# A macaron decoder trunk on one core: the opening taken by token tiles, and the final norm's reciprocal root taken by ScalarE

## The chip, the core and the metric

The kernel runs on 1 core of one Trainium2 chip. The metric is the device time of one execution in microseconds (us), the median over runs; lower is better. Engines are named as the profile names them: PE (TensorE matmul), PEld (its weight loads), DVE (VectorE), ACT (ScalarE), POOL (GpSimd), SP (SyncE, which issues most DMAs; SPq is its queue).

## What is computed

Two layers of a decoder trunk on x of 512 tokens by 1024 features, all float32, then a last RMSNorm:

```python
def rms_norm(x, g):
    y = x * lax.rsqrt(jnp.mean(x * x, axis=-1, keepdims=True) + 1e-6)
    return y * g
def swiglu(x, w_in, w_out):          # w_in 1024 x 5632, w_out 2816 x 1024
    g, u = jnp.split(x @ w_in, 2, axis=-1)
    return (jax.nn.silu(g) * u) @ w_out
h = x
for i in range(2):
    h = h + 0.5 * swiglu(rms_norm(h, ffn1_norm[i]), ffn1_w_in[i], ffn1_w_out[i])
    hn = rms_norm(h, mix_norm[i])
    h = h + (recurrent_mixer(hn, ...) if i == 0 else spatial_gating_mixer(hn, ...))
    h = h + 0.5 * swiglu(rms_norm(h, ffn2_norm[i]), ffn2_w_in[i], ffn2_w_out[i])
return rms_norm(h, final_norm)
```

## The kernel before, in words

**Products.** Every large product is a Strassen-like scheme of seven block products (P1, P2, P5, P6, P3, P7, Q4; `seven`), and every block product is made of three fp32r matmuls per tile (128 x 128 by 128 x 512): both operands are split into a high part `hi` and a rest `lo`, and hi*hi, lo*hi and hi*lo are summed in PSUM. The high part of a weight tile (`whi`) is an ACT copy, its rest (`wlo`) a DVE subtraction (`Sub.split`, recorded at L96 and L87). The left operand is x, transposed on PE by matmuls with the identity into PSUM (tiles `e`, L267), then multiplied with the norm's gain while it is read out of PSUM: `hi` by ACT, `lo` by DVE (L93). x's tokens are the left blocks A11, A12, A22, A21: token tiles 0 and 1 or 2 and 3, first or second 512 features. A block has two groups (`first.g[0]`, `first.g[1]`) of two feature tiles (index q) each.

**Order of the work.** The schedule is manual: each engine executes its instructions in the order in which the program writes them. The list `subs` holds one entry for each weight tile of 128 x 1024 with its matmuls; the loop at the end goes through them, splits up to three entries ahead, and runs hooks tied to an entry's number and phase ("pre" and "mid" ahead of its matmuls, "rest" next to them, "end" behind them). Weights come through 8 buffers (`raw`); SP issues their loads in list order.

**The opening** (from L1411). SP issues one load of x's A11 (tiles 0 and 1 together, 512 KB), then the first weight tile as two halves of 256 KB (`raws[0].halves`), the second weight tile, A12, and more weights. PE runs warm-up matmuls on zeros (L1444), turns the gain, runs three more warm-ups, transposes A11 into two PSUM tiles of one bank each, one per group (`turn(0, "A11")`, `turn(1, "A11")`: group 0's tile holds token tiles 0 and 1 of its two feature tiles), and runs one more warm-up. Then come group 0's first feature tile (`part(0, "A11", 0, True)`: high part and rest both by DVE), the first half of the first weight tile, group 0's second feature tile, the second half of the weight; after six matmuls of P1 `other_block` gives group 1's parts and the second weight tile. P1's matmuls are at L369, those of P2 at L381 to L383, those of the FFN's narrow pair (which comes behind P2, subs[4] to subs[11]) at L828. After P1's second half the block's plain values are needed again: at subs[2] "pre" `value(0, "A11", True)` and `value(1, "A11", True)` take A11 out of PSUM by DVE (four instructions of 128 x 256), and at "rest" ACT takes A12 (four of 128 x 256). Both are `a` in the profile.

**The end.** `FinalNorm` squares the finished pieces of x on ACT, takes the root of the mean with AF.Sqrt (`root`; tile `fs`), and `newton` on DVE takes the reciprocal (L944) and refines it in one Newton step; then x is scaled and stored. Ten entries before the end a one-element Sqrt makes ACT load its table.

The inner order of the first product reads:

```python
[(q, i, m, s) for q, i in qs for m in range(3) for s in range(2)] if ci == 0
    else [(q, i, m, s) for m in range(3) for q, i in qs for s in range(2)]
...
if n == (4 if ci else 6):
    opening[ci]()
```

(s is the token tile, q the feature tile, m = 1 takes x's rest, m = 2 the weight's rest.)

Of the kernel before, what the change touches and what calls it, by code (L numbers as in the profile page):

```python
# [52 lines left out]
def trunk(ctx: ExitStack, tc: tile.TileContext, a: dict, out: bass.AP):  # L53
# [57 lines left out]
    class Raw:  # L111


        halves = False

# [17 lines left out]
        def fetch(self):  # L133
            for q in ((slice(0, 1), slice(1, 2)) if self.halves else (slice(0, self.shape[1]),)):
                nc.sync.dma_start(out=self.v[:, q, :], in_=self.src[:, q, :])

        def add(self, src):
# [200 lines left out]
    def seven(block, cuts, left, w, posts, order=None, own=False, apart=False, joined=None, opening=None):  # L338
# [12 lines left out]
        def mm_of(prod, ci):  # L351
# [3 lines left out]
            def mm(sub):  # L355
# [6 lines left out]
                if opening and prod == "P1":  # L362
                    qs = list(enumerate(pairs))
                    for n, (q, i, m, s) in enumerate([(q, i, m, s) for q, i in qs for m in range(3) for s in range(2)]
                                                     if ci == 0 else
                                                     [(q, i, m, s) for m in range(3) for q, i in qs for s in range(2)]):
                        if n == (4 if ci else 6):
                            opening[ci]()
                        nc.tensor.matmul(bk[name, s], left(prod, i, s)[m == 1], (sub.lo if m == 2 else sub.hi)[:, q, :],  # L369
                                         start=(i, m) == (0, 0), stop=(i, m) == (cuts[-1][-1], 2))  # L370
                    for s in range(2 * ci):
                        posts[prod](s, bk[name, s])
                    return
# [524 lines left out]
    class FinalNorm:  # L898
# [32 lines left out]
        def root(self, t, n):  # L931

            g, i = t // 2, t % 2
            if g not in self.s:
                self.s[g] = self.new("fs", 2)
            act(self.s[g][:, i : i + 1], self.q[g, n][:, i : i + 1], AF.Sqrt, bias=self.m[g][:, i : i + 1])

        def newton(self, g, n, i):
# [4 lines left out]
            tt(v, q, m, ALU.add)  # L943
            nc.vector.reciprocal(out=r, in_=r)  # L944
            if w == 1:
# [460 lines left out]

    hook(len(subs) - 10, "rest", lambda: act(tiny(1), vcol(0), AF.Sqrt))

# [7 lines left out]

    def load_x(t0, c0, w=512):
        src = a["x"][0][t0 * P : (t0 + 2) * P, c0 : c0 + w]
        nc.sync.dma_start(out=X[:, t0 : t0 + 2, c0 : c0 + w], in_=src.rearrange("(t p) c -> p t c", p=P))

# [7 lines left out]

    raws[0].halves = True
    load_x(0, 0)  # L1430
    load_more(2)
# [41 lines left out]

    def part(i, name, q, vector=False):

        g, c, gain = first.g[i], slice(q * H, (q + 1) * H), first.src(i, name)[1][q]
        if name not in g.hl:
            g.hl[name] = slot(F32R, "hi"), slot(F32R, "lo")
        hi, lo = (t[:, c] for t in g.hl[name])
        src = opening[i, name][:, c]  # L1480
        if vector:
            ts(hi, src, gain, None, ALU.mult)
        else:
            act(hi, src, AF.Copy, scale=gain)
        stt(lo, src, gain, f32(hi), ALU.mult, ALU.subtract)

    def value(i, name, vector=False):

        g, ps, gains = first.g[i], opening.pop((i, name)), first.src(i, name)[1]
        if name == "A21" or not vector:  # L1490
            g.take(name, ps, gains)
            return
# [12 lines left out]
    def other_block():  # L1505
        parts(1, "A11")
        subs[1].split()

    warm_up(3, 512)
    turn(0, "A11")  # L1510
    turn(1, "A11")
    warm_up(1, 512)
    part(0, "A11", 0, True)
    subs[0].split(lambda: part(0, "A11", 1))
    for n, phase, fn in ((3, "rest", vec_rest),
                         (2, "pre", lambda: (value(0, "A11", True), value(1, "A11", True))),
                         (2, "rest", lambda: (value(0, "A12"), value(1, "A12"))),
# [63 lines left out]
```

## Time and profile before

| | |
|---|---|
| median of 3 runs | 1608.38 us (1608.36 to 1608.82) |
| the profiled execution's own time | 1609.21 us |
| span inside it | 1606.4 us |
| busy share of the span | PE 99%, PEld 83%, DVE 85%, ACT 65%, POOL 14% |
| mean granted TensorE clock | 0.999 |
| ACT table loads | 23 |

The span runs from the first to the last recorded instruction of the profiled execution; 2.8 us of its own time lie around it. Its own time is 0.83 us over the median. A line of the timeline reads: start in us, duration in us, engine, source line, operation, output<-inputs, shape, and the number of equal instructions merged into the line; in brackets how long the engine had been idle before it and whose result ended that. A merged line lasts from the first start to the last end.

### The profile page before, as it was taken

The numbers are of one execution on the slowest core, as the hardware profiler recorded it, in microseconds if no ns is written. First come the engines' busy times: TensorE is split into PE (matmuls) and PEld (weight loads), VectorE is DVE, ScalarE is ACT, GpSimd is POOL, SyncE is SP. The second block draws the span as 40 slices with busy tenths as digits, with TensorE's granted clock in tenths as the row PEclk, the third lists the DMA queues.
The fourth block names the chain that finished last, engine by engine and source line by source line (L and its number), as shares of the span: only waits on it lengthen the run. The fifth ranks groups of instructions, "written<-read, shape, count | busy, mean of one in ns | idle before, by whom it ended". The sixth has DMA issues, their size and how long they took to land.

```text
span 1606.4 us, 20839 instructions
## 1 busy us (share of the span) xinstructions
PE 1598.0 (99%) x7451; PEld 1331.0 (83%) x7451; DVE 1368.8 (85%) x1837; ACT 1036.6 (65%) x1504; POOL 222.3 (14%) x201
## 2 busy tenths in 40 slices
PE   9999999999999999999999999999999999999998
PEld 7888888898888888888888888888888888888886
DVE  6998888888998788878987988878978988879778
ACT  7656556658777556656776565566886766565566
POOL 2111111100011111111101111111211011111110
PEclk9999999999999999999999999999999999999999
DMA  9877876944383886876837768768877657686693
GB/s 289 184 165 166 214 182 153 221 125 112 87 216 83 187 215 156 208 164 161 206 98 182 171 161 214 183 148 213 224 191 193 157 126 189 171 208 160 166 209 97
DMA packets 164263, 279.29 MB, mean 174 GB/s; under 512 B 11472, under 2 KB 37184, under 8 KB 164160
## 3 DMA queue, kind: packets, MB, share of 16 engines
q1 hardware_dynamic: 114656, 184.84, 36.8%
q0 software_dynamic: 47712, 91.30, 34.2%
q10 hardware_dynamic: 1792, 1.84, 0.4%
q8 instruction: 58, 0.95, 0.2%
q14 instruction: 45, 0.37, 0.1%
HBM read 275.84 MB, written 2.10 MB: 173 GB/s over the span
## 4 chain that ended last, share of the span: by engine, by line
PE 98%; DVE 1%; DMA 0%; ACT 0%; issue 0%; SPq 0%; DVEq 0%
PE A L382 14%; PE A L383 14%; PE A L381 14%; PE C L382 8%; PE C L381 8%; PE C L383 8%; PE p L828 5%; PE B L382 4%; PE B L383 4%; PE B L381 4%; PE e L267 4%; PE r L225 2%; PE r L227 2%; PE r L226 2%; PE Q L383 1%; PE Q L382 1%
## 5 line engine op out<-in xcount | busy, mean ns | idle before, releaser
L87 DVE TENSOR_TENSOR wlo<-raw,whi 128x1024 fp32r<-128x1024 f32 (+1 forms) x537 | 640.2, 1194 | 181.9 <-ACT whi L96 176.9
L96 ACT ACTIVATE whi<-raw 128x1024 fp32r<-128x1024 f32 (+1 forms) x537 | 554.9, 1034 | 368.9 <-PE A L382 118.1
L381 PE MATMUL A<-whi,hi 128*128 128x512 f32 x1016 | 399.8, 394 | 0.0
L383 PE MATMUL A<-wlo,hi 128*128 128x512 f32 x1016 | 396.4, 390 | 0.0
L382 PE MATMUL A<-whi,lo 128*128 128x512 f32 x1016 | 396.2, 390 | 0.0
L383 PEld LDWEIGHTS A<-wlo,hi 128*128 128x128 f32 x1016 | 190.8, 188 | 40.0 <-DVE wlo L87 0.4
L382 PEld LDWEIGHTS A<-whi,lo 128*128 128x128 f32 x1016 | 191.0, 188 | 38.4 <-DVE lo L87 0.3
L381 PEld LDWEIGHTS A<-whi,hi 128*128 128x128 f32 x1016 | 191.0, 188 | 38.1
L381 PE MATMUL C<-whi,hi 128*128 128x512 f32 x560 | 218.6, 390 | 0.0
L382 PE MATMUL C<-whi,lo 128*128 128x512 f32 x560 | 218.3, 390 | 0.0
L383 PE MATMUL C<-wlo,hi 128*128 128x512 f32 x560 | 218.2, 390 | 0.0
L138 POOL DMA_DIRECT2D raw<-in_ffn_w_in_dram x82 | 99.1, 1216 | 733.2 <-DVE raw L87 374.3
L138 POOL DMA_DIRECT2D raw<-in_ffn_w_out_dram x72 | 83.4, 1202 | 367.6 <-DVE wlo L87 171.8
L87 DVE TENSOR_TENSOR raw<-raw,raw 128x1024 f32<-128x1024 f32 x108 | 129.9, 1202 | 0.5
L87 DVE TENSOR_TENSOR lo<-a,hi 128x512 fp32r<-128x512 f32 (+1 forms) x188 | 123.4, 663 | 2.2 <-ACT hi L96 2.1
L96 ACT ACTIVATE hi<-a 128x512 fp32r<-128x512 f32 (+1 forms) x188 | 112.0, 601 | 19.6 <-DVE a L87 16.7
L382 PEld LDWEIGHTS C<-whi,lo 128*128 128x128 f32 x560 | 105.2, 188 | 22.3 <-DVE lo L87 0.7
L381 PEld LDWEIGHTS C<-whi,hi 128*128 128x128 f32 x560 | 105.2, 188 | 21.7
L383 PEld LDWEIGHTS C<-wlo,hi 128*128 128x128 f32 x560 | 105.2, 188 | 21.7
L96 ACT ACTIVATE c<-A 128x512 f32<-128x512 f32 x132 | 77.7, 597 | 70.3 <-PE A L383 70.3
L381 PE MATMUL B<-whi,hi 128*128 128x512 f32 x280 | 109.4, 391 | 0.0
L383 PE MATMUL B<-wlo,hi 128*128 128x512 f32 x280 | 109.1, 390 | 0.0
(168 smaller groups left out, 2092.5 us busy)
## 6 DMA issues: line engine op xcount, KB each, us to landing
raw<-in_ffn_w_in_dram SPq DMA_DIRECT2D x161, 512.0 KB, 4.5
raw<-in_ffn_w_out_dram SPq DMA_DIRECT2D x100, 512.0 KB, 5.7
raw<-in_ffn_w_in_dram POOLq DMA_DIRECT2D x82, 512.0 KB, 7.5
raw<-in_ffn_w_out_dram POOLq DMA_DIRECT2D x60, 512.0 KB, 7.8
raw<-in_sg_w_in_dram SPq DMA_DIRECT2D x20, 512.0 KB, 6.7
raw<-in_ffn_w_in_dram SPq DMA_DIRECT2D x34, 256.0 KB, 4.9
raw<-in_rec_w_in_dram SPq DMA_DIRECT2D x16, 512.0 KB, 3.9
raw<-in_sg_w_in_dram POOLq DMA_DIRECT2D x12, 512.0 KB, 8.2
```

Source lines behind the costliest of these rows:

```text
L87: nc.vector.tensor_tensor(out=o, in0=x, in1=y, op=op)
L96: nc.scalar.activation(out=o, in_=x, func=f, **k)
L138: nc.gpsimd.dma_start(out=self.v, in_=src, accum_op=ALU.add)
L225: nc.tensor.matmul(ps, wh, xh, start=start, stop=False)
L226: nc.tensor.matmul(ps, wh, xl, start=False, stop=False)
L227: nc.tensor.matmul(ps, wl, xh, start=False, stop=stop)
L267: nc.tensor.transpose(ps[:, o : o + P], src(q, s), ident)
L381: nc.tensor.matmul(ps, zh, wh, start=fresh and i == 0, stop=False, **k)
L382: nc.tensor.matmul(ps, zl, wh, start=False, stop=False, **k)
L383: nc.tensor.matmul(ps, zh, wl, start=False, stop=end, **k)
L828: nc.tensor.matmul(bank_of(half, s), z, (sub.lo if m == 2 else sub.hi)[:, q, :], start=left[2] == "2" and (h, q, m) == (0, 0, 0), stop=lef ...
```

## The change

x's A11 is loaded as two token tiles of 256 KB each, with the first weight tile's halves between: tile 0, weight half 0, tile 1, weight half 1. Each token tile is transposed by itself into one PSUM bank that holds both groups (`turn_tile`), and split by itself (`part_tile`: two ACT and two DVE instructions of 128 x 128 for each group and token tile). The warm-ups are 1 ahead of tile 0's transposes and 2 behind them, in place of 3 ahead and 1 behind. The program's order is: tile 0 of group 0, tile 0 of group 1, the first weight half, tile 1 of group 0, the second weight half, and after six matmuls tile 1 of group 1 and the second weight tile. P1's first six matmuls go token tile by token tile. `value_tiles` takes A11's plain values in eight pieces of 128 x 128: group 0's four by DVE, group 1's four by ACT. At the end AF.Abs_reciprocal_sqrt stands in place of AF.Sqrt, and DVE's reciprocal is gone.

```diff
@@ -111,7 +111,8 @@
     class Raw:
 
 
-        halves = False
+
+        halves = None
 
         def __init__(self, src, shape, plus=None, wait=2):
             self.src, self.shape, self.plus, self.wait, self.uses, self.done = src, shape, plus, wait, 0, 0
@@ -133,6 +134,8 @@
         def fetch(self):
             for q in ((slice(0, 1), slice(1, 2)) if self.halves else (slice(0, self.shape[1]),)):
                 nc.sync.dma_start(out=self.v[:, q, :], in_=self.src[:, q, :])
+                if self.halves and q.start == 0:
+                    self.halves()
 
         def add(self, src):
             nc.gpsimd.dma_start(out=self.v, in_=src, accum_op=ALU.add)
@@ -361,7 +364,8 @@
                     return
                 if opening and prod == "P1":
                     qs = list(enumerate(pairs))
-                    for n, (q, i, m, s) in enumerate([(q, i, m, s) for q, i in qs for m in range(3) for s in range(2)]
+                    for n, (q, i, m, s) in enumerate([(0, pairs[0], m, s) for s in range(2) for m in range(3)] +
+                                                     [(1, pairs[1], m, s) for m in range(3) for s in range(2)]
                                                      if ci == 0 else
                                                      [(q, i, m, s) for m in range(3) for q, i in qs for s in range(2)]):
                         if n == (4 if ci else 6):
@@ -933,7 +937,7 @@
             g, i = t // 2, t % 2
             if g not in self.s:
                 self.s[g] = self.new("fs", 2)
-            act(self.s[g][:, i : i + 1], self.q[g, n][:, i : i + 1], AF.Sqrt, bias=self.m[g][:, i : i + 1])
+            act(self.s[g][:, i : i + 1], self.q[g, n][:, i : i + 1], AF.Abs_reciprocal_sqrt, bias=self.m[g][:, i : i + 1])
 
         def newton(self, g, n, i):
 
@@ -941,7 +945,6 @@
             w = i.stop - i.start
             v, c = tiny(w), tiny(w)
             tt(v, q, m, ALU.add)
-            nc.vector.reciprocal(out=r, in_=r)
             if w == 1:
                 stt(c, r, v, r, ALU.mult, ALU.mult)
             else:
@@ -1404,7 +1407,7 @@
     hook(len(subs) - 24, "late", last.load)
     hook(len(subs) - 16, "rest", last.halve)
 
-    hook(len(subs) - 10, "rest", lambda: act(tiny(1), vcol(0), AF.Sqrt))
+    hook(len(subs) - 10, "rest", lambda: act(tiny(1), vcol(0), AF.Abs_reciprocal_sqrt))
 
 
     stage = slot(name="stage")
@@ -1414,9 +1417,9 @@
     first_gain = tp.tile([8, P], F32, tag="fgain1", name="first_gain", bufs=1)
     nc.scalar.dma_start(out=first_gain, in_=a["ffn1_norm"][0].rearrange("(n p) -> n p", p=P))
 
-    def load_x(t0, c0, w=512):
-        src = a["x"][0][t0 * P : (t0 + 2) * P, c0 : c0 + w]
-        nc.sync.dma_start(out=X[:, t0 : t0 + 2, c0 : c0 + w], in_=src.rearrange("(t p) c -> p t c", p=P))
+    def load_x(t0, c0, nt=2):
+        src = a["x"][0][t0 * P : (t0 + nt) * P, c0 : c0 + 512]
+        nc.sync.dma_start(out=X[:, t0 : t0 + nt, c0 : c0 + 512], in_=src.rearrange("(t p) c -> p t c", p=P))
 
     loaded = 0
 
@@ -1426,8 +1429,8 @@
             raws[loaded].load()
             loaded += 1
 
-    raws[0].halves = True
-    load_x(0, 0)
+    raws[0].halves = lambda: load_x(1, 0, 1)
+    load_x(0, 0, 1)
     load_more(2)
     load_x(0, 512)
     load_more(6)
@@ -1471,23 +1474,56 @@
     def parts(i, name):
         first.g[i].direct(name, opening[i, name], first.src(i, name)[1])
 
-    def part(i, name, q, vector=False):
-
-        g, c, gain = first.g[i], slice(q * H, (q + 1) * H), first.src(i, name)[1][q]
-        if name not in g.hl:
-            g.hl[name] = slot(F32R, "hi"), slot(F32R, "lo")
-        hi, lo = (t[:, c] for t in g.hl[name])
-        src = opening[i, name][:, c]
-        if vector:
-            ts(hi, src, gain, None, ALU.mult)
-        else:
-            act(hi, src, AF.Copy, scale=gain)
-        stt(lo, src, gain, f32(hi), ALU.mult, ALU.subtract)
+    class Tiles:
+
+
+        def __init__(self, name):
+            self.of = [slot(F32R, name)[:, :H] for _ in range(2)]
+
+        def __getitem__(self, at):
+            q, t = divmod(at[1].start // P, 2)
+            return self.of[t][:, q * P : (q + 1) * P]
+
+    def turn_tile(t):
+
+        opening["x", t] = ps = aux("e")
+        for i in range(2):
+            src, _ = first.src(i, "A11")
+            for q in range(2):
+                o = (2 * i + q) * P
+                nc.tensor.transpose(ps[:, o : o + P], src(q, t), ident)
+
+    def pieces(i, t):
+
+        return [(opening["x", t][:, (2 * i + q) * P : (2 * i + q + 1) * P], first.src(i, "A11")[1][q]) for q in range(2)]
+
+    def part_tile(i, t):
+        g = first.g[i]
+        if "A11" not in g.hl:
+            g.hl["A11"] = Tiles("hi"), Tiles("lo")
+        hi, lo = ([p.of[t][:, q * P : (q + 1) * P] for q in range(2)] for p in g.hl["A11"])
+        for q, (ps, gain) in enumerate(pieces(i, t)):
+            act(hi[q], ps, AF.Copy, scale=gain)
+        for q, (ps, gain) in enumerate(pieces(i, t)):
+            stt(lo[q], ps, gain, f32(hi[q]), ALU.mult, ALU.subtract)
+
+    def value_tiles():
+        for i, g in enumerate(first.g):
+            g.new("A11")
+            for t in range(2):
+                for q, (ps, gain) in enumerate(pieces(i, t)):
+                    o = g.part("A11", q)[:, t * P : (t + 1) * P]
+                    if i == 0:
+                        ts(o, ps, gain, None, ALU.mult)
+                    else:
+                        act(o, ps, AF.Copy, scale=gain)
+        for t in range(2):
+            del opening["x", t]
 
     def value(i, name, vector=False):
 
         g, ps, gains = first.g[i], opening.pop((i, name)), first.src(i, name)[1]
-        if name == "A21" or not vector:
+        if not vector:
             g.take(name, ps, gains)
             return
         t = g.new(name)
@@ -1503,17 +1539,18 @@
         subs[3].split()
 
     def other_block():
-        parts(1, "A11")
+        part_tile(1, 1)
         subs[1].split()
 
-    warm_up(3, 512)
-    turn(0, "A11")
-    turn(1, "A11")
     warm_up(1, 512)
-    part(0, "A11", 0, True)
-    subs[0].split(lambda: part(0, "A11", 1))
+    turn_tile(0)
+    part_tile(0, 0)
+    part_tile(1, 0)
+    warm_up(2, 512)
+    turn_tile(1)
+    subs[0].split(lambda: part_tile(0, 1))
     for n, phase, fn in ((3, "rest", vec_rest),
-                         (2, "pre", lambda: (value(0, "A11", True), value(1, "A11", True))),
+                         (2, "pre", value_tiles),
                          (2, "rest", lambda: (value(0, "A12"), value(1, "A12"))),
                          (4, "end", lambda: (turn(0, "A22"), turn(1, "A22"))),
                          (5, "mid", lambda: (parts(0, "A22"), parts(1, "A22"))),
```

## Rows read from the trace of the kernel before

**Rows 1.** The page's chain that ended last, by engine.
```profile
PE 98%; DVE 1%; DMA 0%; ACT 0%; issue 0%; SPq 0%; DVEq 0%
```

**Rows 2.** The chain, first 30 us: start us, duration us, what.
```profile
1.31 4.41 DMA raw<-in_ffn_w_in_dram
...
6.43 3.13 PE A L369 x12
...
18.92 2.73 PE p L828 x12
```

**Rows 3.** Timeline of SP's queue, first loads of x and weights.
```profile
0.81 0.44 SPq L1419 DMA_DIRECT2D x<-in_x_dram  x1
1.31 1.41 SPq L135 DMA_DIRECT2D raw<-in_ffn_w_in_dram  x3
```

**Rows 4.** Timeline of PE and its weight loads up to the first product.
```profile
1.26 2.31 PE L1444 MATMUL warm<-warm 128*128 128x512 bf16 x5 [1.26 <-DVE warm L1439]
...
3.71 1.46 PE L1444 MATMUL warm<-warm 128*128 128x512 bf16 x3
...
5.05 0.86 PEld L267 LDWEIGHTS e<-ident,x 128*128 128x128 f32 x8 [0.79 <-DMA x<-in_x_dram]
5.06 1.09 PE L267 MATMUL e<-ident,x 128*128 128x128 f32 x8
```

**Rows 5.** Timeline of ACT, first splits.
```profile
5.74 0.63 ACT L96 ACTIVATE whi<-raw 128x512 fp32r<-128x512 f32 x1 [2.79 <-DMA raw<-in_ffn_w_in_dram]
6.86 0.47 ACT L96 ACTIVATE hi<-e,vec 128x256 fp32r<-128x256 f32 x1 [0.48 <-DVE lo L93]
7.23 0.62 ACT L96 ACTIVATE whi<-raw 128x512 fp32r<-128x512 f32 x1
...
8.46 1.06 ACT L96 ACTIVATE whi<-raw 128x1024 fp32r<-128x1024 f32 x1
```

**Rows 6.** Timeline of DVE, first splits.
```profile
6.28 0.48 DVE L93 SCALAR_TENSOR_TENSOR lo<-e,vec,hi 128x256 fp32r<-128x256 f32 x1
6.68 0.68 DVE L87 TENSOR_TENSOR wlo<-raw,whi 128x512 fp32r<-128x512 f32 x1
...
9.56 1.23 DVE L87 TENSOR_TENSOR wlo<-raw,whi 128x1024 fp32r<-128x1024 f32 x1
```

**Rows 7.** Timeline of ACT, DVE and PE, 12 to 20 us.
```profile
12.69 1.08 ACT L96 ACTIVATE whi<-raw 128x1024 fp32r<-128x1024 f32 x1
13.64 1.10 ACT L96 ACTIVATE c<-A 128x512 f32<-128x512 f32 x2
14.07 1.22 DVE L87 TENSOR_TENSOR wlo<-raw,whi 128x1024 fp32r<-128x1024 f32 x1
14.60 1.60 ACT L96 ACTIVATE a<-e,vec 128x256 f32<-128x256 f32 x4
15.20 1.66 DVE L90 TENSOR_SCALAR a<-e,vec 128x256 f32<-128x256 f32 x4
16.02 2.07 ACT L96 ACTIVATE whi<-raw 128x1024 fp32r<-128x1024 f32 x2
17.18 1.23 DVE L87 TENSOR_TENSOR wlo<-raw,whi 128x1024 fp32r<-128x1024 f32 x1 [0.32 <-ACT whi L96]
...
19.21 0.39 PE L828 MATMUL p<-wlo,hi 128*128 128x512 f32 x1
```

**Rows 8.** Timeline of DVE and ACT around 23.5 us.
```profile
23.00 0.88 DVE L93 SCALAR_TENSOR_TENSOR lo<-e,vec,hi 128x256 fp32r<-128x256 f32 x2
23.91 0.47 ACT L96 ACTIVATE a<-e,vec 128x256 f32<-128x256 f32 x1 [0.22 <-DVE lo L93]
```

**Rows 9.** The chain, its last us: start us, duration us, what.
```profile
1601.20 0.17 DVE fs L944
...
1601.40 0.23 DVE ti L93
```

**Rows 10.** Timeline of ACT, the last table load.
```profile
1574.93 1.28 ACT L96 ACT_TABLE_LOAD   x1
```

## The prediction

> **What bounds the kernel now.** I read the chain that ended last first: PE holds 98% of the span [rows 1]. So a change elsewhere counts only where PE starts its products, where it later runs dry, and behind its last matmul. The chain's beginning [rows 2] shows what holds PE at the start: the first weight half lands at 1.31 + 4.41 = 5.72, and the first product starts at 6.43. From there to 9.56 come the twelve matmuls of the first weight tile; they need 12 x 0.2275 = 2.73 (the step of a later dozen [rows 2]), so only 0.4 is lost between them. The opening holds some 6.4 us without a product and little else to gain. The timelines of SP, PE, ACT and DVE [rows 3 to 7] then give who waits for whom. About 0.2% of the time, 3.2 us, is what a measurement of this kernel can tell from no change; all cases below but two lie inside that.
>
> **The loads.** SP issues a load each 0.47 (three in 1.41) [rows 3]; one more load shifts the later issues by 0.47. They have cover: the second weight tile, issued as the fourth load, before 2.8, is split at 8.46 without a wait for a DMA [rows 3, 5]. Bytes and their order stay otherwise the same. x's A11 (512 KB) is at PE at 5.05 [rows 4] and the weight half behind it (256 KB) 0.67 later, so token tile 0 should be there at 5.05 - 0.67 = 4.38. Bounds: 5.05 if halving brings nothing, 3.7 if it comes two such steps earlier. I take 4.38, from the nearest pair of landings; weight half 0 then lands at 5.05, tile 1 at 5.72.
>
> **Transposes of tile 0.** Eight take 1.09 with a step of 0.107 (0.86 for eight loads), the last 0.34 [rows 4]. But the warm-ups ahead of them step 0.425 for 512 columns (2.31 less 1.46 is two steps), twice the 0.2275 of a product: TensorE at 1.2 GHz, although the profile's mean granted clock is near full. Tile 0's transposes now run where those slow warm-ups ran. At the slow pace the fourth ends at 4.38 + 3 x 0.20 + 0.40 = 5.38, at the fast one at 5.04. I take 5.38.
>
> **One pair of splits.** ACT: 128 x 256 from PSUM takes 0.47, and four in a row 1.60, a step of 0.38 [rows 5, 7]; 512 columns more cost 1.06 - 0.63 = 0.43, so 128 fewer save 0.11. A pair of 128 x 128 takes 0.27 + 0.36 = 0.63. DVE: 0.48, step (1.66 - 0.48) / 3 = 0.39, 1.23 - 0.68 = 0.55 for 512 columns; a pair takes 0.25 + 0.34 = 0.59 [rows 6, 7].
>
> **Who may read a bank.** ACT's `hi` at 6.86 had been held 0.48, until DVE's `lo` at 6.28 ended at 6.76 [rows 5, 6]. Two readings fit: the two wrote and read one `hi` slot, or they read one PSUM bank. The second case parts them: ACT's `a` at 23.91 writes a slot of its own, and still waited 0.22 for the two `lo` that end at 23.88; they share only the bank they read [rows 8]. So an ACT read waits for DVE reads of the same bank that stand ahead of it in the program. The Trainium skill (PSUM — Partial Sum Buffer, section on PSUM bank collisions) says that two engines must not touch one bank in one partition at once, reads against reads included; by the slot reading the sum would be that of the first rival below, by the page's it is the one that follows.
>
> **First product.** The new tile puts both groups into one bank, and group 1's pair stands ahead of the weight half on ACT. In steps, with 0.04 for each handover: ACT's pair for group 0 5.42 to 6.05; DVE's pair 6.09 to 6.68; ACT's pair for group 1 6.72 to 7.35; weight half 0 from 7.25 to 7.88 (an ACT instruction starts 0.10 before the last ends, as at 7.23 [rows 5]); first matmul 7.94, as 0.06 passed before. That is 1.51 later than 6.43, though the weight half has lain there since 5.05.
>
> **To P1's second half.** DVE's rest of weight half 0 ends at 8.60, the third matmul waits for it until 8.65, the other nine follow at 0.2275: the twelve are through at 10.93. ACT meanwhile: group 0's tile 1 7.78 to 8.41, weight half 1 to 8.94, then group 1's tile 1 must wait for DVE's pair (8.61 to 9.20) and lasts to 9.87, the second weight tile to 10.83. PE and ACT meet at 10.93, against 9.56 before: +1.37. Taking tile by tile in the first six matmuls hides nothing of this, and one warm-up fewer lies in PE's idle time. The four slots more cost nothing: the pool turns over 60, and no row here waits for a slot.
>
> **The plain values.** This is where the end is set. DVE's four of 128 x 256 (1.66) become four of 128 x 128 (1.09), and ACT gets four, 4 x 0.27 = 1.08, ahead of A12's. Again both read the same banks, DVE first. A12's parts, gated by PE, and the fourth weight tile (12.69) move by 1.35 to 14.04, so it ends at 15.12; DVE takes its rest from 15.16 instead of 14.07, +1.09, and the plain values from 15.20 + 1.09 = 16.29: tile 0's pair to 16.88, tile 1's to 17.38. ACT, free at 16.0, waits: pairs at 16.92 and 17.45, then A12's values at 17.95 instead of 14.60, +3.35 [rows 7]. Queued behind them on ACT is the fifth weight tile (16.02 to 19.37), behind that DVE's rest of it (17.18 to 20.53). Before, that rest ended at 18.41 and its first reader on PE started at 19.21 [rows 7], 0.75 to spare after the handover. PE is therefore late by 3.35 - 0.75 = 2.60 here, which takes in the 1.37. The next weight tile has over 2 us to spare (another dozen and eight transposes lie between), and from there PE is never dry.
>
> **The end.** Each reciprocal on the final chain costs 0.20 from its start to the next instruction's [rows 9]. Three stand in the tail; PE's last matmuls and the last square cover the first two, so 0.2 goes; bounds 0 and 0.6. The root itself stays one ACT instruction, and its table is still loaded far ahead, at 1574.93 [rows 10].
>
> **Sum.** +2.60 - 0.2 = +2.4. On the profiled execution: a span of 1606.4 becomes 1608.8, its own time 1609.21 becomes 1611.6. That execution lies 0.83 above the median of the runs, 1608.38, so I put the sum on the median: 1610.8. With the bounds (transposes fast -0.34, landing -0.68 or +0.67, tail) its own range is 1609.7 to 1611.7.
>
> **Rivals.**
> - **No wait between the readers.** Then group 1's pair follows at once and the first matmul comes 0.67 earlier, P1's second half at about +0.7; ACT's 1.08 of values delays the fifth weight tile by 1.8, less 0.75 is +1.0, with the tail +0.8: 1609.2. For it: the 6.86 row alone could be the slot. Against: rows 8.
> - **Faster: the opening does what its order suggests.** Tile 0 lands at 3.7, transposes run fast, and four ACT pieces (3 x 0.27 + 0.36 = 1.17) end at 5.57 without waiting; weight half 0 is split by 6.10, the first matmul comes at 6.16, P1's second half at 9.13 (-0.43), and the added 1.08 on ACT fits into the 0.75 and that gain. With the tail -0.6: 1607.7. It decides where ACT's first weight split starts before 5.74. Against: it needs an early landing and no bank wait.
> - **Slower by more: PE's pace falls.** Between tile 1's transposes (done by about 6.4) and 7.94 PE idles 1.5 us that were filled before. If P1's first twelve then run at the warm-ups' 0.425, that adds 12 x 0.2 = 2.4; with six, 1.2; all behind it shifts along: 1612.0 to 1613.2. For it: the warm-ups show that the slow pace lasts until about 5 us. Against: transposes and warm-ups still keep PE active from 3.7 to 6.4. The Trainium skill (TensorE: Matmul & The Clock Gate, Part 1) says the clock is given by how busy TensorE has lately been; by that rule this rival could come true, and no row here shows PE idle at that point.
> - **The new root isn't as cheap.** If its table lacked copy or square, each change in the tail would cost 1.28 [rows 10], on the final chain four or five, 1614 to 1616. The Sqrt that stands there shows none.
>
> **How the numbers follow.** Forecast 0.62, no wait 0.10, faster opening 0.13, slow pace 0.12, tables 0.03. The forecast's time is 1610.8. The range reaches from the faster opening's value, 1607.7, to the lower part of the slow pace, 1612.3; outside lie half of the one, half of the other, the tables and a little of the forecast. Faster by over 0.2% (under 1605.2) needs more than any case gives: 0.01. Slower by over 0.2% (over 1611.6): slow pace, tables and 0.05 of the forecast, 0.20. Within: 0.79.
>
> **What would show it.** Right: ACT's first weight split at about 7.2, not waiting for a DMA; ACT's `hi` and `a` of group 1 with idle time released by DVE; a first product at 7.9; a hole in PE of some 1 us at the third matmul at L828, released by `wlo`; no reciprocal at L944. Wrong: a first matmul before 6.5, ACT reading a bank while DVE reads it, or PE not dry at L828.

## The result, and the profile after

The changed kernel takes 1611.70 us (median of 16 runs, 1610.59 to 1612.74) against 1608.72 for the kernel before (16 runs beside them, 1608.34 to 1609.62): a ratio of 1.0018, 95% interval 1.0010 to 1.0026. It is 2.98 us slower. The profiled execution took 1611.54, of which 1609.7 are its span; before, 1609.21 and 1606.4.

The timeline of ACT after the change (start in us, duration in us; it answers to [rows 5] and [rows 7]):

```profile
5.21 0.63 ACT L96 ACTIVATE hi<-e,vec 128x128 fp32r<-128x128 f32 x2 [2.28 <-PE e L1494]
6.51 0.63 ACT L96 ACTIVATE hi<-e,vec 128x128 fp32r<-128x128 f32 x2 [0.68 <-DVE lo L93]
7.03 0.63 ACT L96 ACTIVATE whi<-raw 128x512 fp32r<-128x512 f32 x1
...
8.94 0.63 ACT L96 ACTIVATE hi<-e,vec 128x128 fp32r<-128x128 f32 x2 [0.24 <-DVE lo L93]
9.45 1.06 ACT L96 ACTIVATE whi<-raw 128x1024 fp32r<-128x1024 f32 x1
11.23 1.06 ACT L96 ACTIVATE whi<-raw 128x1024 fp32r<-128x1024 f32 x1 [0.71 <-DMA raw<-in_ffn_w_in_dram]
...
13.87 1.08 ACT L96 ACTIVATE whi<-raw 128x1024 fp32r<-128x1024 f32 x1
...
16.81 2.60 ACT L96 ACTIVATE a<-e,vec 128x128 f32<-128x128 f32 x8 [0.89 <-DVE a L90]
19.27 2.98 ACT L96 ACTIVATE whi<-raw 128x1024 fp32r<-128x1024 f32 x3
...
1123.45 1.99 ACTq L1201 DMA_DIRECT2D vg<-in_sg_v_norm_dram  x1
```

Three of ACT's instructions that read PSUM stand idle in front and are released by DVE: 0.68 ahead of group 1's pair, 0.24 ahead of its second tile, 0.89 ahead of the plain values. The first, with the two pairs that now stand ahead of it, delays the weight half, split at 7.03 instead of 5.74; the last, with the four values put on ACT, delays the fifth weight tile, at 19.27 instead of 16.02.

DVE's timeline (it answers to [rows 6] and [rows 7]):

```profile
5.87 0.61 DVE L93 SCALAR_TENSOR_TENSOR lo<-e,vec,hi 128x128 fp32r<-128x128 f32 x2 [1.89 <-ACT hi L96]
...
16.17 1.12 DVE L90 TENSOR_SCALAR a<-e,vec 128x128 f32<-128x128 f32 x4
...
20.39 1.23 DVE L87 TENSOR_TENSOR wlo<-raw,whi 128x1024 fp32r<-128x1024 f32 x1 [3.10 <-ACT whi L96]
```

DVE waits 3.10 for ACT's split of the fifth weight tile, where it waited 0.32 [rows 7].

PE's timeline, and its weight loads further on (it answers to [rows 4] and [rows 7]):

```profile
3.71 0.61 PE L1447 MATMUL warm<-warm 128*128 128x512 bf16 x1
4.11 1.06 PE L1494 MATMUL e<-ident,x 128*128 128x128 f32 x4
...
6.84 0.63 PE L1494 MATMUL e<-ident,x 128*128 128x128 f32 x4 [1.04 <-DMA x<-in_x_dram]
7.71 0.50 PE L373 MATMUL A<-whi,hi 128*128 128x512 f32 x1 [0.23 <-ACT whi L96]
...
10.87 1.08 PE L373 MATMUL A<-whi,hi 128*128 128x512 f32 x4
...
21.67 0.50 PE L832 MATMUL p<-wlo,hi 128*128 128x512 f32 x1 [0.53 <-DVE wlo L87]
...
55.97 0.85 PEld L270 LDWEIGHTS e<-ident,h 128*128 128x128 f32 x8 [0.43 <-PE A L387]
```

And the chain that ended last, its last us (it answers to [rows 9]):

```profile
1604.36 0.30 ACT fs L96
1604.69 0.23 DVE ti L93
```

ACT's root now releases DVE's Newton step directly; the reciprocal between them is gone.

Where the same PE instruction starts in both profiles, after less before, says where the time goes:

| place on PE | later by | step |
|---|---|---|
| P1's second half, 9.58 -> 10.87 | 1.29 | 1.29 |
| first matmul of the narrow pair, 18.76 -> 20.41 | 1.65 | 0.36 |
| its third matmul, 19.21 -> 21.67 | 2.46 | 0.81 |
| the matmul behind it, 19.44 -> 22.01 | 2.57 | 0.11 |
| transposes of h, 53.20 -> 56.00 | 2.80 | 0.23 |
| products from 1128.7 us on | 3.46 | 0.66 |
| last matmul, 1598.91 -> 1602.45 | 3.54 | 0.08 |
| from there to the end of the span, 7.49 -> 7.27 | 3.32 | -0.22 |

Most of the loss is made in the first 22 us. The 0.66 near 1125 us belongs to this execution alone: an ACT DMA issue took 1.99 where the other twelve profiles show 0.53 to 1.18, and none of the others shifts there.

### The profile page after: what moved, and what is told of

Read it like the earlier page. It is cut to its first block, busy times and chain, and to the rows that moved or that the text cites. A ratio compares the mean times of both kernels' runs of the same rounds, so it can differ in the third digit from the quotient of the medians.

```text
span 1609.7 us, 20851 instructions
## 1 busy us (share of the span) xinstructions
PE 1599.0 (99%) x7450; PEld 1330.5 (83%) x7450; DVE 1367.9 (85%) x1837; ACT 1039.1 (65%) x1513; POOL 222.7 (14%) x201
## 4 chain that ended last, share of the span: by engine, by line
PE 97%; ACT 1%; DVE 1%; DMA 0%; issue 0%; ACTq 0%; SPq 0%; DVEq 0%
PE A L386 14%; PE A L387 14%; PE A L385 14%; PE C L385 8%; PE C L386 8%; PE C L387 8%; PE p L832 5%; PE B L386 4%; PE B L387 4%; PE B L385 4%; PE e L270 4%; PE r L228 2%; PE r L229 2%; PE r L230 2%; PE Q L386 1%; PE Q L385 1%
```

## The experiments

A kernel with a median and an interval was timed in three or five rounds beside the kernel before; the others are single executions, and one of those can lie 0.5 to 0.8 off by PE's pace in the opening (e2). Their readings go by where PE's instructions start. In code and rows, a line of three dots stands for lines that are not shown.

**e1_root_alone.** The kernel before with the new root and without the reciprocal.

```diff
-            act(self.s[g][:, i : i + 1], ..., AF.Sqrt, bias=...)
+            act(self.s[g][:, i : i + 1], ..., AF.Abs_reciprocal_sqrt, bias=...)
...
-            nc.vector.reciprocal(out=r, in_=r)
```

> The kernel before with the new root alone. Theory (the reciprocal leaves the tail, nothing else moves): the opening's rows as before (first product at 6.4, third matmul at the pair at 19.2), from the last matmul's start to the end of the span about 7.25 us instead of 7.49, ratio to before 0.9999 (0.9995 to 1.0002). Rival (the new root's table lacks copy or square): table loads of 1.28 us in the last 15 us, 4 to 6 us more.

Median 1608.10 (10 runs) against 1608.71, ratio 0.9999 (0.9989 to 1.0008). From the last matmul's start to the end it takes 7.24 instead of 7.49, that is -0.25, and no table load is added (23 in both). The chain's last us show why it is one reciprocal: the root's 0.30 is followed at once by the Newton step.

```profile
1601.02 0.30 ACT fs L96
1601.35 0.23 DVE ti L93
```

So the root part is worth about 0.2, too little for its own timing to show, and the whole loss is the opening's.

**e2_values_act_first.** The changed kernel with ACT's plain values written ahead of DVE's.

```diff
-        for i, g in enumerate(first.g):
+        for i, g in reversed(list(enumerate(first.g))):
```

> The changed kernel with group 1's plain values (ACT) written ahead of group 0's (DVE). Theory (ACT waits for DVE's reads of the same bank that stand ahead of it): ACT's 0.89 us of idle time ahead of the values goes, its values start at 15.9 instead of 16.8, the fifth weight tile at 18.4 instead of 19.27, the third matmul of the pair at about 20.8 instead of 21.67, so 0.9 us of the loss goes; DVE's four wait instead, without cost. Rival (only the added ACT work counts, the wait is of another origin): the fifth weight tile stays at 19.2 and the third matmul at 21.6.

ACT's timeline:

```profile
16.63 2.64 ACT L96 ACTIVATE a<-e,vec 128x128 f32<-128x128 f32 x8
19.06 3.06 ACT L96 ACTIVATE whi<-raw 128x1024 fp32r<-128x1024 f32 x3
```

DVE's:

```profile
17.33 1.13 DVE L90 TENSOR_SCALAR a<-e,vec 128x128 f32<-128x128 f32 x4 [0.27 <-ACT a L96]
```

Turned round, the wait changes sides: ACT's values follow its copies without idle time, and DVE waits 0.27. Nothing but the order of the reads differs, so the wait is one between two readers of one bank. But the time hardly fell (1610.66, against a lowest of 1610.59 for the changed kernel); this execution ran P1's first matmuls at half the pace:

```profile
8.30 0.63 PE L373 MATMUL A<-whi,lo 128*128 128x512 f32 x1
8.73 0.63 PE L373 MATMUL A<-wlo,hi 128*128 128x512 f32 x1
```

The step is 0.43 per 512 columns instead of 0.23, until about 10; P1's second half comes 2.16 late instead of 1.29. Read from there, the values add little: the pair's third matmul is at 21.53, 2.32 late, so 0.16 more than P1's second half, where the changed kernel adds 1.17. That reading is weak, because a later PE also leaves ACT more time: the fifth weight tile is split at 19.06, only 0.21 earlier than in the changed kernel, where 18.4 had been expected. So e2 shows whose wait it is, not what it costs.

**e3_act_pairs_first.** The changed kernel with both of ACT's pairs for tile 0 written ahead of both of DVE's.

```diff
-    part_tile(0, 0)
-    part_tile(1, 0)
+    part_both(0)
```

(`part_both` takes `hi` of groups 0 and 1 by ACT, then `lo` of both by DVE.)

> The changed kernel with ACT's two pairs for tile 0 written ahead of DVE's two pairs. Theory (bank order): ACT's idle 0.68 us between the pairs goes, the first weight split starts at 6.3 instead of 7.03, the first product at 6.95 instead of 7.71; P1's second half gains less, since tile 1's transposes wait until 6.8 for their load: 10.5 to 10.9. Rival (ACT waits there for something else, a slot or a load): first weight split still at 7.0, first product 7.7.

ACT's timeline, then PE's:

```profile
5.17 1.15 ACT L96 ACTIVATE hi<-e,vec 128x128 fp32r<-128x128 f32 x4 [2.24 <-PE e L1494]
6.19 0.65 ACT L96 ACTIVATE whi<-raw 128x512 fp32r<-128x512 f32 x1
...
11.80 1.06 ACT L96 ACTIVATE whi<-raw 128x1024 fp32r<-128x1024 f32 x1 [1.20 <-DMA raw<-in_ffn_w_in_dram]
```
```profile
7.05 0.63 PE L1494 MATMUL e<-ident,x 128*128 128x128 f32 x4 [1.49 <-DMA x<-in_x_dram]
7.44 0.47 PE L373 MATMUL A<-whi,hi 128*128 128x512 f32 x1
```

The first bank wait is gone and the weight half is split 0.84 earlier. The first product gains only 0.27: tile 1's transposes stand ahead of it on PE, and their load landed at 6.92. The opening thus has two walls of nearly one height: ACT's wait, and behind it tile 1's landing. P1's second half comes at 10.74, 0.13 earlier than in the changed kernel. Yet the pair's third matmul is 3.02 late, 0.56 more than there: in this execution the third weight tile landed at 11.78 instead of 11.20, and ACT waits 1.20 for it. So its time, 1611.21, does not say what the bank wait is worth.

**e4_before_one_load_more.** The kernel before with one more load of 4 KB on SP's queue, for the theory that one more load shifts something far behind (the 0.66 near 1125 us).

```diff
+    more = tp.tile([8, P], F32, tag="more", name="more", bufs=1)
+    nc.sync.dma_start(out=more, in_=a["ffn1_norm"][0]...)
```

> The kernel before with one more load of 4 KB on SP behind the opening's loads, which nothing reads. Theory (the loads of SP and ACT take turns on a few completion semaphores, so one load more pairs every later load with another earlier one): opening as before, PE without shift up to 1128 us, there about 0.7 us late, because ACT's last load at L1198 waits about 2 us instead of 0.54: span about 1607.1. Rival (that stall of the changed kernel comes from its late ACT or DVE, not from the count of loads): no shift anywhere, span 1606.4.

1608.80; no shift at 1128 us. That theory fell: ACT's issue takes 0.89 here, not the 2 that had been expected.

**e6_values_dve.** The changed kernel with all eight plain values on DVE.

```diff
-                    if i == 0:
-                        ts(o, ps, gain, None, ALU.mult)
-                    else:
-                        act(o, ps, AF.Copy, scale=gain)
+                    ts(o, ps, gain, None, ALU.mult)
```

> The changed kernel with all eight plain values of 128 x 128 on DVE, none on ACT. Theory (the wait for DVE's reads and ACT's 1.1 us of added work delay the fifth weight tile, and with it the pair): ACT's A12 values start right behind the two copies at 15.8, the fifth weight tile at about 17.3 instead of 19.27, the third matmul of the pair is late by no more than P1's second half is (1.2 to 1.4 at full pace) instead of by 2.46: 1.1 less, ratio to before about 1.0009. Rival (the late loads set the pair's start): the third matmul stays 2.2 or more behind, ratio 1.0015 or more.

Median 1609.65 (10 runs), ratio 1.0007 (0.9997 to 1.0016): 2.05 less than the changed kernel. The spans of its runs, 1607.0 to 1608.2, all lie under the lowest of the changed kernel, 1608.8. ACT's timeline, then PE's:

```profile
16.53 1.61 ACT L96 ACTIVATE a<-e,vec 128x256 f32<-128x256 f32 x4
17.96 3.02 ACT L96 ACTIVATE whi<-raw 128x1024 fp32r<-128x1024 f32 x3
```
```profile
11.63 1.08 PE L373 MATMUL A<-whi,hi 128*128 128x512 f32 x4
...
21.16 0.39 PE L832 MATMUL p<-wlo,hi 128*128 128x512 f32 x1
```

The profiled execution ran P1 at the slow pace too (second half at 11.63, 2.05 late), yet the pair's third matmul is 1.95 late, not later than P1. So giving four values to ACT, behind DVE's reads, is what loses time at the pair. How that divides between the wait and the work, no run shows in time; e7 bears on it.

**e7_before_values_act.** The kernel before with group 1's values by ACT. There the two groups lie in banks of their own, so ACT gets the added work without the added wait.

```diff
-                         (2, "pre", lambda: (value(0, "A11", True), value(1, "A11", True))),
+                         (2, "pre", lambda: (value(0, "A11", True), value(1, "A11"))),
```

> The kernel before with group 1's plain values by ACT (two of 128 x 256 from a bank of its own) instead of by DVE. Theory (what costs in the changed kernel is the shared bank's wait, 0.9, on top of ACT's added work, which the 0.75 us of slack nearly covers): ACT without idle time ahead of them, the fifth weight tile 0.75 later, at 16.8, the pair's third matmul late by 0 to 0.1. Rival (ACT's added work alone empties the slack): late by 0.5 or more.

ACT's timeline, then PE's:

```profile
15.15 2.33 ACT L96 ACTIVATE a<-e,vec 128x256 f32<-128x256 f32 x6
17.29 3.03 ACT L96 ACTIVATE whi<-raw 128x1024 fp32r<-128x1024 f32 x3
```
```profile
19.76 0.48 PE L828 MATMUL p<-wlo,hi 128*128 128x512 f32 x1
```

1608.88. The first product, at 6.98, is 0.55 late, mostly because the transposes ran slowly in this execution (1.97 against 1.09), and the pair's third matmul is 0.55 late as well: two instructions more on ACT add nothing. The fifth weight tile starts 1.27 later than before, of which 0.55 came with the opening; the other 0.7 fits into the 0.75 that the prediction had read as spare there. Here the work without the wait is hidden; in the changed kernel the work with a wait of 0.89 on top is not.

**e8_after_one_x_load.** The changed kernel with x's A11 in one load of 512 KB again.

```diff
-    raws[0].halves = lambda: load_x(1, 0, 1)
-    load_x(0, 0, 1)
+    raws[0].halves = lambda: None
+    load_x(0, 0, 2)
```

> The changed kernel with A11 loaded in one piece of 512 KB as before, all else as changed. Theory (the first small load lands early, and the alternating small loads then run slower, about 230 GB/s from 3.6 to 6.4 us where the kernel before has 330 to 370): x lands at 5.0, weight half 0 at 5.7, the second weight tile at 7.7 instead of 8.6, the third at 10.2 instead of 11.2, ACT does not wait for it; the first product at 8.2 instead of 7.71, P1's second half at 11.1, the pair's third matmul about as late as in the changed kernel, 2.4 to 2.9. Rival (the slow stretch is that execution's alone): the same landings in this kernel as in the changed one's other executions.

1612.44; x lands at 5.19, the weight halves at 5.93 and 6.58, the second weight tile at 8.80, the third at 11.36. The loads behind x did not come back to the landings before (7.70 and 10.24), which had been expected: their lateness is not tied to the split of x. The first product is at 8.88, 1.17 later than with tile loads: tile 0's transposes start at 5.23 instead of 4.11, ACT's first pair at 6.38 instead of 5.21, and ACT's chain sets the product as before. So within this order loading x by tiles is a gain for the first product; what it is worth in time, this single execution does not say.

**e10_more_warm_ups.** The changed kernel with five warm-ups instead of two ahead of tile 1's transposes.

```diff
-    warm_up(2, 512)
+    warm_up(5, 512)
```

> The changed kernel with five warm-ups between the two tiles' transposes instead of two, which fill PE's idle time ahead of tile 1's load. Theory (in some executions the first product runs at the warm-ups' pace of 0.43 for 512 columns because PE idles just ahead, which spreads the times from 1610.6 to 1612.7): the profiled first product steps 0.23, the highest of the times comes down towards 1611.5, the median falls by 0.3 to 0.6 to about 1611.2. Rival (the pace depends on where the execution stands when PE begins, not on these 2 us): the same spread and median as without, 1611.7.

Median 1611.65 (10 runs), ratio 1.0019 (1.0010 to 1.0028). Nothing changed, against the expectation of 0.3 to 0.6 less: PE's idle time in the opening is not what the change costs.

**e11_weight_half_first.** The kernel before with the new root, the first weight half loaded and split ahead of x, and group 1's parts ahead of group 0's second feature tile.

```diff
-    raws[0].halves = True
-    load_x(0, 0)
+    raws[0].halves = lambda: load_x(0, 0)
...
-    part(0, "A11", 0, True)
-    subs[0].split(lambda: part(0, "A11", 1))
+    subs[0].split(first_parts)
```

(`first_parts` takes group 0's first feature tile, group 1's parts, then group 0's second feature tile; `other_block` loses group 1's parts.)

> The kernel before with the new root, the first weight half loaded ahead of x (a first load of 256 KB landed at 3.6 in the changed kernel) and split ahead of x's parts; group 1's parts stand ahead of group 0's second feature tile, so that ACT reads its bank while DVE reads the other. Theory (the opening is bound by ACT's order and by who reads which bank): first weight split at 3.7, x at 5.0 to 5.7, first product 6.3 to 6.9, ACT's second weight tile from 7.8 instead of 8.46, P1's second half at 9.2 to 9.6 instead of 9.58; with the root 0.2 to 0.6 us less than before, ratio 0.9996 to 1.0. Rival (x is late by the whole weight half, and the first product with it): x at 5.7, first product 6.9, P1's second half 9.6 to 10, no gain.

Median 1609.65 (11 runs), ratio 1.0005 (0.9997 to 1.0014): no gain. The half is split at 3.59, but x lands at 5.85 instead of 5.01, its transposes ran slowly (1.97 against 1.09), and the first product, at 7.72, waits for them.

**e12_x_tiles_first.** e6 with x's two tile loads back to back, ahead of the weight halves.

```diff
-    raws[0].halves = lambda: load_x(1, 0, 1)
+    raws[0].halves = lambda: None
     load_x(0, 0, 1)
+    load_x(1, 0, 1)
```

> The changed kernel with all values on DVE and with x's two tiles loaded one behind the other, ahead of the weight's halves. Theory (the slow stretch comes with alternating x and weight in small loads): tile 1 lands at about 4.4, the weight halves at 5.1 and 5.7, the third weight tile at 10.2 to 10.5, and the first product stays at 7.7, held by ACT's order. Rival (it comes with the number of small loads at the start): weight halves at 6.5 and 7.2, the third weight tile at 11.2 or later as in the changed kernel.

1609.09. Tile 1 now lands at 4.86 and its transposes are over by 5.7, so the wall that e3 found is out of the way, and the first one stands alone. ACT's timeline, then PE's:

```profile
6.20 0.62 ACT L96 ACTIVATE hi<-e,vec 128x128 fp32r<-128x128 f32 x2 [0.68 <-DVE lo L93]
```
```profile
7.39 0.50 PE L373 MATMUL A<-whi,hi 128*128 128x512 f32 x1 [1.67 <-ACT whi L96]
```

PE has both tiles and waits 1.67 for the weight half, which waits on ACT behind the bank. What had been expected of the loads did not come: the weight halves land at 5.90 and 6.54, between the two theories, and the third weight tile at 11.91, the latest of all profiles.

**e13_group_1_later.** e12 with group 1's tile 0 moved behind the first matmuls, to its tile 1.

```diff
     def other_block():
+        part_tile(1, 0)
         part_tile(1, 1)
...
     part_tile(0, 0)
-    part_tile(1, 0)
```

> As e12, and group 1's pair for tile 0 stands behind the second weight half instead of ahead of the first. Theory (that pair, with its wait for DVE, is what holds the first weight split): ACT's first weight split starts at 5.8 or when its half lands, instead of 7.03, the first product 0.6 to 1.2 earlier, at 6.5 to 7.1; P1's second half at 10.0 to 10.4; total 1609.0 to 1609.4, ratio about 1.0004. Rival (the pair's place does not matter, the second weight tile behind it holds P1's second half anyway): P1's second half at 10.8 as in the changed kernel, total as with the values on DVE alone, 1609.65.

ACT's timeline, then that of PE and its weight loads:

```profile
5.11 0.62 ACT L96 ACTIVATE hi<-e,vec 128x128 fp32r<-128x128 f32 x2 [2.18 <-PE e L1495]
5.62 0.63 ACT L96 ACTIVATE whi<-raw 128x512 fp32r<-128x512 f32 x1
...
10.87 1.06 ACT L96 ACTIVATE whi<-raw 128x1024 fp32r<-128x1024 f32 x1 [1.61 <-DMA raw<-in_ffn_w_in_dram]
```
```profile
6.30 0.50 PE L373 MATMUL A<-whi,hi 128*128 128x512 f32 x1 [0.36 <-ACT whi L96]
...
9.47 1.09 PE L373 MATMUL A<-whi,hi 128*128 128x512 f32 x4
...
13.64 0.19 PEld L386 LDWEIGHTS B<-whi,lo 128*128 128x128 f32 x1 [0.56 <-DVE lo L93]
...
19.44 0.39 PE L832 MATMUL p<-wlo,hi 128*128 128x512 f32 x1
```

Median 1608.44 (10 runs) against 1608.67, ratio 0.9999 (0.9990 to 1.0008). The first product is 0.13 earlier than before the change, P1's second half 0.11 earlier; the pair's third matmul is 0.23 later. What was gained is lost again at P2. The third weight tile lands at 10.85 (before 10.24), ACT waits 1.61 for it, DVE's `lo` of A12 comes behind that, and PE's second matmul of P2 waits for this `lo`: P2's first matmul is 0.21 early (13.11 for 13.32), its third 0.20 late (13.98 for 13.78). So with neither bank wait left, the opening by token tiles loses a little by a late load, and the new root gives about as much back. No version tried beats the kernel before by more than the measurement can tell.

**The account.** In medians of the time the change costs 2.98, and e6 takes 2.05 of it back. The spans of the single executions lie closer together than their times and part the kernels better:

| kernel | executions | span, median (lowest to highest) |
|---|---|---|
| before | 53 | 1606.8 (1606.4 to 1607.9) |
| e1, the new root alone | 10 | 1606.4 (1606.2 to 1606.9) |
| changed | 16 | 1609.45 (1608.8 to 1610.7) |
| e10, more warm-ups | 10 | 1609.45 (1609.1 to 1610.0) |
| e6, values on DVE | 10 | 1607.15 (1607.0 to 1608.2) |
| e13, loads and group 1's place too | 10 | 1606.75 (1606.2 to 1607.3) |

By the spans the change costs 2.65. The plain values' place is 2.3 of it (1609.45 to 1607.15). The loads' order and the place of group 1's tile 0 together are 0.4 (1607.15 to 1606.75), where the medians of the time say 1.21. The opening of e13 still stands 0.35 over the root alone, which is worth 0.2 to 0.4. How the 0.4 divides is not shown: e12 is one execution, and in the profiles the place of group 1's tile is worth 1.05 at P1's second half (10.52 to 9.47).

## Why the prediction was right, and where it was not

**The mechanism.** Right in both places. The prediction chose the bank reading over the slot reading from [rows 8], and e2, e3 and e13 confirm it: with the order of the reads turned, or with the second reader moved away, the idle time ahead of ACT's instruction goes, while each writes a tile of its own. No run parts the bank from the PSUM tile: each `e` fills one bank. And a releaser in a row is inferred from a semaphore, so what the rows show is an order that the program keeps. The Trainium skill (PSUM — Partial Sum Buffer, section "PSUM bank collisions raise a hardware error") says that the compiler's scheduler adds a dependency between instructions of two engines that touch one bank in the same partitions, reads as well as writes; the trace agrees, with 0.68, 0.24 and 0.89 us.

**First product, P1's second half.** Forecast at 7.94 and 10.93, measured at 7.71 and 10.87. ACT's pairs and the weight half came at 5.21, 6.51 and 7.03 instead of 5.42, 6.72 and 7.25, all some 0.21 early. That it is so little is luck: tile 0 landed 0.76 earlier than reckoned (3.62 for 4.38), but its transposes start only at 4.11, behind the warm-up at 3.71, and took 1.06 for the 1.00 reckoned. Each duration of the chain (0.63 for ACT's pair, 0.61 for DVE's against the 0.59 reckoned) held.

**The plain values, where the end is set.** Forecast: ACT's values at 16.92, the fifth weight tile at 19.37, its rest at 20.53, PE late by 2.60 at the pair's third matmul. Measured: 16.81, 19.27, 20.39, and 2.46 there, 2.57 one matmul further. e7 shows the other half of that step in the order before: added work alone, up to the 0.75 to spare, costs nothing.

**The tail.** -0.2 forecast, -0.22 in the changed kernel and -0.25 in e1.

**What failed: the loads.** "I take 4.38" was a landing worked out from two loads in a row. Tile 0 landed at 3.62, past the bound that had been set for the good side (3.7), while tile 1 came at 6.71 instead of 5.72 and the weights behind it about 0.95 later than before (the third tile at 11.20, before 10.24). That tile 1 came late did not set the first product, which waits 0.23 for ACT; it is the wall behind, which e3 shows. "They have cover" was read from the second weight tile alone. For the third, ACT already waited before the change:

```profile
10.26 1.06 ACT L96 ACTIVATE whi<-raw 128x1024 fp32r<-128x1024 f32 x1 [0.73 <-DMA raw<-in_ffn_w_in_dram]
```

After it ACT waits 0.71, for a load that lands 0.96 later, and the chain that ended last runs through this load. Before, it ran on PE alone from the first product on [rows 2]. From the chain after:

```profile
3.65 7.55 DMA raw<-in_ffn_w_in_dram
...
12.32 0.13 DVE wlo L87
...
15.03 0.08 DVE wlo L87
```

From there it goes to DVE's plain values at 16.17, to ACT's at 16.81 and to the fifth weight tile. The path that the prediction reckoned with, over PE and ACT's split of the fourth weight tile, was done at 14.95 (13.87 + 1.08), within 0.1 of it. So in this profile the late load adds next to nothing to the 2.46. In other executions it does: in e3 and e10 the third tile landed at 11.78 and 11.69, ACT waited 1.20 and 1.15 for it, and the pair's third matmul came 3.02 and 2.94 late although P1's second half came earlier (10.74 and 10.82). What the loads cost in the median, no run separates.

**What failed: "from there PE is never dry".** It loses 0.11 at the next matmul and 0.23 near 56 us, where transposes of h wait. PE had come 2.57 late but DVE, which has no idle time there, about 3.2 (its first `h` starts at 55.37, before at 52.15); its delay is bigger than PE's and shows as soon as PE needs it. e6, without the values on ACT, has no such loss. This term, some 0.3, was left out of the sum of +2.4. With it and the measured 2.46 and 0.22 the sum is 2.46 + 0.11 + 0.23 - 0.22 = 2.58, near the 2.65 by which the spans differ; 0.4 of the 2.98 in time remain. Executions differ: P1 at the slow pace in some, the third weight tile later than in the changed kernel's profile in most variants, ACT's long issue in the profiled one. Which of these makes the 0.4 is open.

**The time and its range.** The forecast, 1610.8, was put on a median of three executions, 1608.38; the sixteen beside the changed kernel gave 1608.72. So 0.34 of the 0.90 by which 1611.70 lies above it is the kernel before, not the change. By the bounds that the sum lists, its own range begins at 1609.4, not at 1609.7. And 0.2% was too wide for what a measurement here can tell: the interval of the ratio is 0.0008 to either side, and +0.18% is clear of it.

**The rivals.** *No wait between the readers*: fell by the rows. *Faster opening*: its condition, ACT's first weight split before 5.74, is met by one kernel with tile loads, e13 (5.62), which takes them in another order, and by e11 (3.59), which loads the weight half first; neither is faster than before. *PE's pace falls*: the prediction gave it as an alternative. It is a thing of single executions: the changed kernel's profile and e10's have P1 at 0.23 a step, e2's and e6's at 0.43 up to about 10. It is not bound to the change, as e4's and e7's transposes, in the order before, ran slowly too (0.5 late). The Trainium skill (TensorE: Matmul & The Clock Gate, Part 1) lets the clock follow recent activity; no run here shows that as the cause, as e10's added warm-ups changed nothing, and after 1.04 us of idle time the changed kernel's transposes ran at the full pace (0.63 for four, against 1.08 in e2 after 0.49). *New tables*: none was added (23 loads in both).

## What to carry to other kernels

ACT and DVE, reading one PSUM bank, took turns here in the order in which the program wrote their reads (ACT idle 0.89; turned round in e2, DVE idle 0.27): group the reads by engine, the engine with the fuller queue first, or give each reader's data a bank of its own. A small piece put ahead of an item on a full queue costs its wait and its own time, less what that item had to spare, so find what is queued behind it before judging its size. When an opening is reordered, expect a second wall directly behind the first: here the bank wait, the landing of tile 1 and the place of group 1's piece had all to go before P1's second half was on time, and behind it stood the landing of the third weight tile. And follow the chain that ended last through the profile after, not only the rows that were forecast: here it ran through a load that the forecast had called covered.

## What was not expected of the hardware

Loads in the first microseconds do not follow one rate. The windows view of PE (stretch, its length, PE's busy time, granted clock, DMA share, GB/s moved) shows it, first for the kernel before, then for the changed one:

```profile
3.30:5.00 1.70, 1.70 (x5) 1.00 0.97 330
5.00:6.40 1.40, 1.37 (x10) 1.00 1.02 369
```
```profile
3.30:5.00 1.70, 1.70 (x8) 1.00 0.96 249
5.00:6.40 1.40, 0.80 (x3) 1.00 0.89 228
```

With 256 KB loads of x and weights in turn, the DMA engines are nearly as busy and move a quarter less in the first stretch and 38% less in the second. In the second, the five profiles with such loads (changed, e2, e3, e6, e10) move 157 to 228, the eight others 284 to 373. That is not all of it: e12, with x's tiles back to back, moves 366 there, but 255 from 7.7 to 9.0, where the kernel before moves 405. The first 256 KB land at 3.5 to 3.6 in the changed kernel, e11, e12 and e13, where 512 KB landed at 5.0 to 5.3. The third weight tile lands at 10.24 to 10.78 in the kernel before, e1, e4 and e7, and at 10.85 to 11.91 in all others, e8 with its whole x among them: why it is late there stays open.

PE's pace and the granted clock part in the opening: e2's P1 matmuls step 0.43 from 7.7 to about 10, the 1.2 GHz level, while the same window grants 1.00, as it does for the changed kernel at 0.23. e2's window:

```profile
7.70:9.00 1.30, 1.29 (x3) 1.00 1.03 395
```

And the same small DMA issue on ACT's queue, of the mixer's gains, took between 0.53 and 1.99 us from one execution to the next; the 1.99 cost PE 0.66, and none of the others, up to 1.18, cost PE anything there.
